# A merge projection fed with fp32 operands in place of split parts, in a two-layer hybrid encoder

## Chip, cores and metric

One core of one Trainium2 chip. The time is device microseconds of one execution of the whole two-layer trunk; runs of a kernel are summed up by their median. The engines are TensorE (PE, its weight loads shown as PEld), VectorE (DVE), ScalarE (ACT), GpSimd (POOL) and SyncE (SP), which issues most transfers.

## The reference

The trunk works on 512 tokens of width 1024. In each of two layers three branches (attention, a long convolution, gated linear attention) make 512 channels each; each branch is projected to 1024, weighted by its own sigmoid gate, and the sum is projected once more and added to the residual. Cross-attention and an MLP follow.

```python
for i in range(DEPTH):
    hn = rmsnorm(h, ln_mix[i])
    (aq, ak, av, hy, gq, gk, gv, go, glr, gates) = split_cols(hn @ w_in[i], IN_SPLITS)
    y_a = attention_mixer(aq, ak, av, attn_qnorm[i], attn_knorm[i], cos, sin) @ w_br_attn[i]
    ...
    y_b = hyena_mixer(hy, hy_conv[i], spec, hy_skip[i]) @ w_br_hyena[i]
    y_c = gla_mixer(gq, gk, gv, go, glr, gla_w_lr[i], gla_b_lr[i], gla_onorm[i]) @ w_br_gla[i]
    gate = jax.nn.sigmoid(gates.reshape(B, L, N_BRANCH, D_MODEL))
    mixed = gate[:, :, 0] * y_a + gate[:, :, 1] * y_b + gate[:, :, 2] * y_c
    h = h + mixed @ w_out[i]
```

All inputs and the output are fp32. The product that the change touches is `attention_mixer(...) @ w_br_attn[i]`: (512 x 512) by (512 x 1024).

## The kernel before

Activations lie with channels on the 128 partitions and the 512 tokens along the free axis. Nearly every large product is made of operands in two parts: `split` (lines 234 to 237) makes a high part in the format fp32r with a cast on ACT, and the rest, also fp32r, with a subtraction on DVE. `mm3` (lines 249 to 253) then accumulates three matmuls of these parts in place of one product: high by high (line 251), high weights' remainder and activations' remainder each by the other's high part (lines 252 and 253).

Weights come in chunks of 512 rows by 256 columns, stored so that a chunk is one transfer of 512 KB into a tile of 128 x 1024 fp32. Three rings of fixed tiles serve the chunks of the whole kernel in turn, in program order: 2 tiles `wr` for what a transfer brings, 3 tiles `wh` and 3 tiles `wl` for its parts (`wbuf`, line 208). `wchunk` (line 264) issues the transfer on SP and the split, the split with a priority that lies 200 steps ahead. `load` (line 256) issues other transfers on SP after the last weight transfer. `proj_cm` (line 296) runs `mm3` over the contraction tiles for one block of 128 output channels.

The work of a layer's mixing part is cut into streams: `at` attention, `gp` and `gh` gated linear attention, `hy0` and `hy1` the two halves of the long convolution, `ga0` to `ga2` the gates, `me0` to `me2` the merges of the three branches, `wo` the output projection, and others. Each stream is a generator, and `weave` (line 1136) advances them in an order written out by hand (`ORDER0`, `ORDER`, lines 145 to 156). `me0`, the merge of the attention branch, has four steps, one for each chunk of weights; three stand among the steps of the convolution and one late, before the merge of the convolution. That is the program order. From it, from the priorities (`AHEAD`, `LATE`) and from its own costs the framework plans the order of the instructions on each engine when the kernel is built.

`attention` (line 425) ends for each pair of heads with a tile of 128 channels by 512 tokens: the sum over the parts of the values into `op` (line 576), the reciprocal sums of the softmax turned round on PE (line 587), a multiplication on DVE (line 589), and a split into `yah` and `yal` (line 591, through lines 235 and 236). `merge` (line 1101) takes the four split tiles, projects them chunk by chunk, and multiplies by the gates on DVE.

```python
BUFS = dict(rb=1, mr=4, gate=8, po=1, p=4, pt=4, op=2, xk=2, xv=2, kvb=3, kvs=6, sw=3, xn=16, h8=8, y=11,
        s12=12, wraw=3, f8=8, ab4=1, F=4, g=14, st=7, wr=2, wh=3, wl=3, tiny=18, vec=2, rn=4, row=1, xg=1, w12=1,
...
    mm(out, lh, rh, start=start, stop=False, skip_group_check=True)
    mm(out, lh, rl, start=False, stop=False, skip_group_check=True)
    mm(out, ll, rh, start=False, stop=stop, skip_group_check=True)
```

Two small products elsewhere use plain fp32 operands, the position features' network of the convolution's filters (lines 646 and 649), and so do the sums over partitions by a column of ones (line 1270 among them).

Of the kernel before, what the change touches and what calls it, by code (L numbers as in the profile page):

```python
# [18 lines left out]
P = 128  # L19
# [74 lines left out]
def laid_out(a):  # L94
# [43 lines left out]
    for s_ in range(2):  # L138
# [29 lines left out]
            kt=300, pt=100, pv=150, qt=200, xs=200, xt=35, xv=10)  # L168
# [6 lines left out]
class Trunk:  # L175
# [101 lines left out]
    def proj_mem(self, W, hp, X, own):  # L277
# [15 lines left out]
                    self.mm3(ps[mt], X[kt][0][..., tk], X[kt][1][..., tk], hi[:, k], lo[:, k], kt == 0, kt == 7)  # L293
        return ps

    def proj_cm(self, ps, w, cols, X):
        n = len(X)
        for kt in range(n):
            hi, lo = w[kt // 4]
            self.mm3(ps, hi[:, kt % 4, cols], lo[:, kt % 4, cols], X[kt][0], X[kt][1],  # L300
                     kt == 0, kt == n - 1)
# [123 lines left out]
    def attention(self, l):  # L425
        nc, W = self.nc, self.I["w_in"][l]
# [33 lines left out]
        w = self.wchunk(W, CKV)  # L460
# [17 lines left out]
        for j in range(2):  # L478
            w = self.wchunk(W, CQ + j)
# [16 lines left out]
        for t in range(NT):  # L496
            qt = q[t].rearrange("p (h d) -> p h d", d=64)
            nc.vector.tensor_tensor(qt, qt, sc[:, 8 * t:8 * t + 8].unsqueeze(2).to_broadcast([P, 8, 64]),
                                    op=ALU.mult)
# [14 lines left out]
        for g in range(2):  # L514
            K2 = KS[g]
            for hh in range(4):
# [22 lines left out]
                for tp in range(2):  # L539
# [12 lines left out]
                    for kp in range(2):  # L552
# [8 lines left out]
                        for k in range(2):  # L561
                            kt = 2 * kp + k
# [7 lines left out]
                    if tp == 0:  # L570
                        yield
                if h % 2 == 0:
                    opair = self.t("op", name="op")
                tmp = self.t("st", name="ot")
                nc.scalar.copy(tmp[64:128], po[64:128])
                nc.vector.tensor_tensor(opair[r], po[0:64], tmp[64:128], op=ALU.add)
                if h % 2 == 1:

                    rs = self.tiny(2 * NT, "rs").rearrange("p (t e) -> p t e", e=2)
                    nc.vector.reciprocal(rs, sums)  # L580
                    wide = self.t("st", (P, NT, 2, 64), F32, "wide")
                    self.engs("aw")[0].tensor_copy(wide.rearrange("p t e d -> p (t e) d"),
                                                   rs.rearrange("p t e -> p (t e)").unsqueeze(2).to_broadcast([P, 8, 64]))
                    pb = self.ps("b")
                    for t in range(NT):
                        with self.late("ab"):
                            nc.tensor.transpose(pb[:, t * P:(t + 1) * P],
                                                wide[:, t].rearrange("p e d -> p (e d)"), self.ident)
                    nc.vector.tensor_tensor(opair, opair, pb, op=ALU.mult)
                    self.dump("ya", opair, lambda d, i=h // 2: d[l, i])  # L590
                    self.ya.append(self.split_new(opair, "y", name="ya"))
                yield


# [506 lines left out]
    def merge(self, l, i, W, last):  # L1101
        nc = self.nc
        y = (self.ya, self.yb, self.yc)[i]
        for mc in range(4):
            w = self.wchunk(W[l], mc, ng=1)
            for j in range(2):
                m = 2 * mc + j
                py = self.ps("mm")
                self.proj_cm(py, w, slice(j * P, (j + 1) * P), y)
                t = self.gate[i][m]  # L1110
                if i == self.first:
                    a = self.t("h8", name="acc")
                    nc.vector.scalar_tensor_tensor(a, t, 1.0, py, op0=ALU.add, op1=ALU.mult)
                    self.acc.append(a)
                else:
                    nc.vector.scalar_tensor_tensor(t, t, 1.0, py, op0=ALU.add, op1=ALU.mult)
                    nc.vector.tensor_tensor(self.acc[m], self.acc[m], t, op=ALU.add)
                if last:
                    self.mixed.append(self.split_new(self.acc[m], "g", name="mix", lo_tag="s12"))
            yield  # L1120
# [337 lines left out]
```

## Time and profile before

| what | value |
|---|---|
| median of 3 runs | 2230.19 us (2228.43 to 2230.83) |
| the profiled execution | 2230.03 us, span 2228.3 us from the first to the last instruction |
| PE busy | 2181.0 us, 98% of the span, 11032 matmuls |
| PE weight loads | 1824.3 us, 82% |
| DVE, ACT, POOL busy | 1532.3 us (69%), 1003.8 us (45%), 197.1 us (9%) |
| mean granted TensorE clock | 0.993 of 2.4 GHz |
| transfers | 233.55 MB, mean 105 GB/s |

Matmuls overlap in their pipeline and their ends are modelled, so the busy time of PE counts some of it twice in neighbouring records; the distance between two starts is what a matmul holds the engine for. A line number of a split or of `mm3` is that of the helper; the names of the tiles tell whose work it is.

### The profile page before, as it was taken

The page shows a single profiled execution, that of the slowest core. Times are in us where ns is not written, and L with a number is a line of the kernel's source. Part 1 is how long each engine was busy: PE and PEld are TensorE (multiplying, and loading weights), DVE is VectorE, ACT ScalarE, POOL GpSimd, SP SyncE. Part 2 cuts the span into 40 slices and gives each one's busy share as a digit, 9 for nine tenths or more (in the row PEclk, how much of TensorE's full clock was granted, in tenths as well). Part 3 has the DMA queues.
Part 4 walks back from the last instruction along what each step waited for, and adds up shares of the span by engine and source line. Part 5 has one row for each costly group of instructions (what it writes and reads, how often), then busy time and mean ns, then how long its engine had stood idle before and what let it go on. Part 6 is the DMA issues. An engine that isn't in the chain of part 4 may idle for free.

```text
span 2228.3 us, 28873 instructions
## 1 busy us (share of the span) xinstructions
PE 2181.0 (98%) x11032; PEld 1824.3 (82%) x11032; DVE 1532.3 (69%) x2615; ACT 1003.8 (45%) x1623; POOL 197.1 (9%) x193
## 2 busy tenths in 40 slices
PE   7989999999999999999999999999999999999999
PEld 5878888887788878888887978888887888888887
DVE  7799866979866656775485795658897575344445
ACT  6656844333344544443335576443333454432231
POOL 2020001000010200000060120110000101000004
PEclk9999999999999999999999999999999999999999
DMA  6432223223242333333344311242233312333332
GB/s 235 151 124 92 65 81 124 67 85 125 78 141 92 102 103 119 125 117 103 97 156 140 100 58 57 76 135 78 81 109 123 133 57 86 95 95 104 95 96 94
DMA packets 80097, 233.55 MB, mean 105 GB/s; under 512 B 9174, under 2 KB 11222, under 8 KB 79960
## 3 DMA queue, kind: packets, MB, share of 16 engines
q1 hardware_dynamic: 76792, 225.95, 31.6%
q0 software_dynamic: 3168, 5.77, 0.9%
q8 instruction: 86, 1.41, 0.3%
q14 instruction: 51, 0.42, 0.1%
HBM read 214.91 MB, written 16.78 MB: 104 GB/s over the span
## 4 chain that ended last, share of the span: by engine, by line
PE 83%; DVE 6%; ACT 3%; DMA 2%; issue 1%; ACTq 0%; DVEq 0%; SPq 0%
PE ps L251 26%; PE ps L253 25%; PE ps L252 25%; DVE wl L236 2%; PE ps L557 1%; ACT wh L235 1%; PE ps L566 1%; PE ps L568 1%; DMA wr<-in_w_in_dram 1%; PE ps L544 1%; ACT p L549 1%; DMA wr<-in_w_br_gla_dram 1%; PE ps L545 1%; PE ps L1312 0%; DVE ab L968 0%
## 5 line engine op out<-in xcount | busy, mean ns | idle before, releaser
L235 ACT CAST wh<-wr 128x1024 fp32r<-128x1024 f32 (+1 forms) x328 | 341.6, 1042 | 518.6 <-PE ps L252 420.6
L236 DVE TENSOR_TENSOR wl<-wr,wh 128x1024 fp32r<-128x1024 f32 x324 | 402.2, 1242 | 250.9 <-ACT wh L235 245.5
L251 PE MATMUL ps<-xh,wh 128*128 128x512 f32 x1344 | 529.8, 395 | 1.7 <-ACT wh L235 1.7
L253 PE MATMUL ps<-xh,wl 128*128 128x512 f32 x1344 | 527.5, 393 | 3.3 <-DVE wl L236 3.1
L252 PE MATMUL ps<-xl,wh 128*128 128x512 f32 x1344 | 528.5, 393 | 0.0
L253 PEld LDWEIGHTS ps<-xh,wl 128*128 128x128 f32 x1344 | 253.2, 188 | 57.5 <-DVE wl L236 6.7
L251 PEld LDWEIGHTS ps<-xh,wh 128*128 128x128 f32 x1344 | 253.4, 189 | 54.4 <-ACT wh L235 2.6
L252 PEld LDWEIGHTS ps<-xl,wh 128*128 128x128 f32 x1344 | 253.5, 189 | 49.2
L253 PE MATMUL ps<-hdh,wl 128*128 128x512 f32 x512 | 199.4, 390 | 0.0
L252 PE MATMUL ps<-hdl,wh 128*128 128x512 f32 x512 | 199.4, 390 | 0.0
L251 PE MATMUL ps<-hdh,wh 128*128 128x512 f32 x512 | 199.2, 389 | 0.0
L1374 DVE TENSOR_TENSOR macc<-ps,macc 128x512 f32<-128x512 f32 x96 | 66.3, 691 | 85.4 <-PE ps L253 84.9
L251 PEld LDWEIGHTS ps<-hdh,wh 128*128 128x128 f32 x512 | 96.1, 188 | 19.9
L252 PEld LDWEIGHTS ps<-hdl,wh 128*128 128x128 f32 x512 | 96.1, 188 | 19.8
L253 PEld LDWEIGHTS ps<-hdh,wl 128*128 128x128 f32 x512 | 96.1, 188 | 19.7
L352 POOL TENSOR_TENSOR hsum<-hsum,hsq 128x512 f32<-128x512 f32 x30 | 43.3, 1445 | 602.4 <-ACT hsq L350 602.4
L251 PE MATMUL ps<-wh,xh 128*128 128x256 f32 x320 | 92.2, 288 | 0.1
L252 PE MATMUL ps<-wl,xh 128*128 128x256 f32 x320 | 91.8, 287 | 0.0
L253 PE MATMUL ps<-wh,xl 128*128 128x256 f32 x320 | 91.6, 286 | 0.0
L1358 DVE TENSOR_TENSOR rl<-rl 128x512 f32<-128x512 f32 x64 | 44.1, 689 | 63.4 <-ACT rl L1357 63.4
L1376 POOL TENSOR_TENSOR macc<-macc,rb 128x512 f32<-128x512 f32 x16 | 23.5, 1467 | 651.1 <-DVE macc L1374 651.1
L1357 ACT ACTIVATE rl<-ps 128x512 f32<-128x512 f32 x64 | 38.0, 593 | 77.8 <-PE ps L253 77.8
(402 smaller groups left out, 4312.5 us busy)
## 6 DMA issues: line engine op xcount, KB each, us to landing
wr<-in_mlp_w_dram SPq DMA_DIRECT2D x128, 512.0 KB, 3.6
wr<-in_w_in_dram SPq DMA_DIRECT2D x108, 512.0 KB, 3.7
wraw<-in_x_wv_dram SPq DMA_DIRECT2D x16, 512.0 KB, 5.8
wr<-in_x_wk_dram SPq DMA_DIRECT2D x16, 512.0 KB, 3.6
F<-ff SPq DMA_DIRECT2D x32, 256.0 KB, 3.0
F<-F SPq DMA_DIRECT2D x32, 256.0 KB, 4.6
wr<-in_w_out_dram SPq DMA_DIRECT2D x16, 512.0 KB, 3.7
wr<-in_x_wq_dram SPq DMA_DIRECT2D x16, 512.0 KB, 3.7
```

The costliest lines, as they stand in the source:

```text
L235: r = self.nc.scalar.copy(hi, src)
L236: (lo_eng or self.nc.vector).tensor_tensor(lo, src, hi, op=ALU.subtract)
L251: mm(out, lh, rh, start=start, stop=False, skip_group_check=True)
L252: mm(out, lh, rl, start=False, stop=False, skip_group_check=True)
L253: mm(out, ll, rh, start=False, stop=stop, skip_group_check=True)
L352: eng.tensor_tensor(self.hsum, self.hsum, sq, op=ALU.add)
L544: nc.tensor.matmul(s, QH[:, tk], K2, start=True, stop=False)
L545: nc.tensor.matmul(s, QL[:, tk], K2, start=False, stop=True)
L1357: nc.scalar.activation(r, ps, AF.Relu)
L1358: nc.vector.tensor_tensor(r, r, r, op=ALU.mult)
L1374: nc.vector.tensor_tensor(acc[m], ps, acc[m], op=ALU.add)
L1376: nc.gpsimd.tensor_tensor(acc[m], acc[m], rb, op=ALU.mult)
```

## The change

The attention branch's tiles are no longer split, and neither are its merge weights. The pair's tile is taken from pool "y" and handed on as it is; `merge` loads the chunk with a new function `wfull`, ordered after the last weight transfer, and passes the fp32 tile `wr` and the fp32 pair tile straight to the matmul, one call for each contraction tile. The merges of the other two branches stay as they are.

```diff
+    def wfull(self, W, n):
+
+        w = self.wbuf("wr")
+        with self.after(self.last_w):
+            self.last_w = self.nc.sync.dma_start(w, W[n, 0])
+        return w.rearrange("p (k n) -> p k n", k=4)
...
                 if h % 2 == 0:
-                    opair = self.t("op", name="op")
+                    opair = self.t("y", name="op")
...
-                    self.ya.append(self.split_new(opair, "y", name="ya"))
+                    self.ya.append(opair)
...
         for mc in range(4):
-            w = self.wchunk(W[l], mc, ng=1)
+            full = i == 0
+            w = self.wfull(W[l], mc) if full else self.wchunk(W[l], mc, ng=1)
             for j in range(2):
                 m = 2 * mc + j
                 py = self.ps("mm")
-                self.proj_cm(py, w, slice(j * P, (j + 1) * P), y)
+                if full:
+                    for kt in range(4):
+                        nc.tensor.matmul(py, w[:, kt, j * P:(j + 1) * P], y[kt], start=(kt == 0), stop=(kt == 3))
+                else:
+                    self.proj_cm(py, w, slice(j * P, (j + 1) * P), y)
```

## Rows read from the trace of the kernel before

**Rows 1.** The page: busy time by engine, and the ending chain by line.

```profile
PE 2181.0 (98%) x11032; PEld 1824.3 (82%) x11032; DVE 1532.3 (69%) x2615; ACT 1003.8 (45%) x1623; POOL 197.1 (9%) x193
...
PE ps L251 26%; PE ps L253 25%; PE ps L252 25%; DVE wl L236 2%; PE ps L557 1%; ACT wh L235 1%; PE ps L566 1%; PE ps L568 1%; DMA wr<-in_w_in_dram 1%; PE ps L544 1%; ACT p L549 1%; DMA wr<-in_w_br_gla_dram 1%; PE ps L545 1%; PE ps L1312 0%; DVE ab L968 0%
```

**Rows 2.** Stretches: length, then busy us of PE, PEld, DVE, ACT, POOL; clock, DMA.

```profile
130.00:640.00 510.00, 495.41 (x2702) 417.83 (x2701) 413.87 (x730) 248.93 (x430) 35.25 (x42) 1.00 0.30 95
...
1260.00:1740.00 480.00, 470.62 (x2516) 395.12 (x2515) 362.63 (x613) 225.58 (x381) 33.90 (x40) 0.99 0.29 91
...
200.00:300.00 100.00, 97.11 (x648) 85.66 (x647) 88.28 (x162) 75.14 (x158) 1.56 (x1) 1.00 0.25 81
470.00:570.00 100.00, 97.26 (x497) 81.70 (x495) 92.18 (x158) 33.26 (x48) 0.00 (x0) 1.00 0.32 100
```

**Rows 3.** Waits of PE, first in 130 to 640 us, then 1260 to 1740.

```profile
PE ps L695 <- ACT w3h L677: 2.9, 1, 2.9
...
PE ps L251 <- ACT wh L235: 0.3, 1, 0.3
...
PE ps L251 <- ACT wh L235: 3.1, 4, 1.5
```

**Rows 4.** Groups by line and form, PE: the merge's first of three.

```profile
L251 PE MATMUL ps<-yah,wh 128*128 128x512 f32 x64 | 25.3, 396 | 0.0
```

**Rows 5.** Timeline of PE at the second merge chunk: start, duration, instruction.

```profile
436.35 0.39 PE L251 MATMUL ps<-yah,wh 128*128 128x512 f32 x1
...
441.79 0.39 PE L251 MATMUL ps<-xh,wh 128*128 128x512 f32 x1
```

**Rows 6.** Line 646: records, shortest, median and longest in ns.

```profile
L646 PE MATMUL ps<-z,consts x4: 589/614/640, 40.1 to 796.2; 33*64 33x512 f32 x4
```

**Rows 7.** Timeline of PE around line 646 in the second layer.

```profile
795.35 0.39 PE L253 MATMUL ps<-xh,wl 128*128 128x512 f32 x1
795.67 1.07 PE L646 MATMUL ps<-z,consts 33*64 33x512 f32 x2
796.67 0.50 PE L251 MATMUL ps<-xh,wh 128*128 128x512 f32 x1
797.00 0.39 PE L252 MATMUL ps<-xl,wh 128*128 128x512 f32 x1
```

**Rows 8.** Timeline of PE at fp32 products with one moving column.

```profile
687.07 0.39 PE L253 MATMUL ps<-xh,wl 128*128 128x512 f32 x1
687.30 0.95 PE L1270 MATMUL ps<-ones,xsq 128*128 128x1 f32 x8
688.11 0.49 PE L251 MATMUL ps<-xh,wh 128*128 128x512 f32 x1
```

**Rows 9.** Splits of weights (the page), then of attention tiles (tile op).

```profile
L235 ACT CAST wh<-wr 128x1024 fp32r<-128x1024 f32 (+1 forms) x328 | 341.6, 1042 | 518.6 <-PE ps L252 420.6
L236 DVE TENSOR_TENSOR wl<-wr,wh 128x1024 fp32r<-128x1024 f32 x324 | 402.2, 1242 | 250.9 <-ACT wh L235 245.5
...
L235 ACT CAST yah<-op x8: 608/620/622, 211.8 to 1504.7; 128x512 fp32r<-128x512 f32 x8
L236 DVE TENSOR_TENSOR yal<-op,yah x8: 681/684/693, 212.4 to 1505.8; 128x512 fp32r<-128x512 f32 x8
```

**Rows 10.** Timeline of SP's queue at the second and fourth merge chunks.

```profile
423.59 0.33 SPq L268 DMA_DIRECT2D wr<-in_w_br_attn_dram  x1
426.53 5.00 SPq L268 DMA_DIRECT2D wr<-in_w_in_dram  x2
...
552.83 3.07 SPq L268 DMA_DIRECT2D wr<-in_w_br_hyena_dram  x2
```

**Rows 11.** Timeline of ACT: casts of the later load of each pair.

```profile
436.90 1.05 ACT L235 CAST wh<-wr 128x1024 fp32r<-128x1024 f32 x1
...
586.43 1.05 ACT L235 CAST wh<-wr 128x1024 fp32r<-128x1024 f32 x1 [6.74 <-PE ps L252]
```

**Rows 12.** Tile wr: time from issue to landing.

```profile
DMA to landing us min/median/max: 1.9/3.6/7.1
```

## The prediction

> **What bounds the kernel now.** I read the page's engine totals and chain first: is one engine the limit? The matrix engine (PE) is busy 98% of the span, and of the chain that ended last 76% lies on the three lines of `mm3` [rows 1]. A busy PE isn't yet a PE that does useful work all the time, so I took the table by stretches next. The attention branch's merge runs in the mixing part of each layer, which lies in 130 to 640 us and 1260 to 1740 us. There PE is busy for 495.41 of 510 us and 470.62 of 480 us, so it idles 14.6 + 9.4 = 24.0 us; VectorE (DVE) is busy 81% and 76%, ScalarE (ACT) 49% and 47% [rows 2]. The waits of PE show how small the pieces of that idle time are: the longest entry of the first stretch is 2.9 us, and a split of weights (`wh`, line 235) makes it wait 0.3 us there and 3.1 us in the second [rows 3]. So work taken from DVE or ACT can give back little, and work added to PE is paid nearly in full.
>
> **How a product of the merge is paid today.** One (128 x 128) by (128 x 512) product is three matmuls of fp32r parts: hi x hi, lo x hi and hi x lo, 64 of each over both layers [rows 4]: 4 column chunks x 2 halves x 4 contraction tiles x 2 layers = 64 products. The record of one lasts 0.39 us, but its end is modelled; what counts is the distance from start to start. The second chunk's merge starts at 436.35 us, the next work at 441.79: 24 matmuls in 5.44 us, 0.2267 us each [rows 5]. A product is 3 x 0.2267 = 0.680 us, the whole merge 64 x 0.680 = 43.5 us of PE.
>
> **What an fp32 product costs.** The trace has no 128 x 128 by 512 product of plain fp32. The nearest is line 646, fp32 operands with 512 moving columns but only 33 rows and 64 columns of weights. Its two calls left four records, so one fp32 product is two matmuls with two weight loads; the records last 589 to 640 ns [rows 6], against 389 for an fp32r one. Three prices follow:
> Lower end: the records' lengths differ by 589 - 389 = 200 ns at the same columns, so a record holds PE 0.2267 + 0.200 = 0.427 us, a product 0.853 us.
> From start to start: the pair at 795.67 us spans 1.07 us, the second record lasts 0.589, so it starts 0.48 us after the first [rows 6, 7]. The first record is 51 ns longer than the second; if that is the wait for a weight load with nothing ahead of it, 0.43 us is left, near the lower end.
> Upper end: on line 646 the surrounding stream is moved further. The start before the pair is at 795.35; without the pair the second start after it would have come 2 x 0.2267 later, at 795.80, and it comes at 797.00 [rows 7]. So the pair cost 1.20 us, with both changes between weight tiles of 64 and 128 columns in it.
> In a chunk 8 fp32 products stand in a row with the same tile as their neighbours, so the edges should mostly go away. That weight loads needn't show: fp32 products of full 128 x 128 weights by one column run in the trace, eight records in 688.11 - 687.30 = 0.81 us, 0.10 us a record, and the first of them starts 0.23 us after an fp32r matmul, on the usual beat [rows 8]. A weight load thus fits four times into a 0.43 us record. I take 0.427 to 0.440 us a record (the second allows the 13 ns by which 0.2267 us is over 512 columns at the granted 2.4 GHz), 0.87 us a product.
> Of this the Trainium skill (page "FP8 and Floating Point Precision", section "TensorE Precision Notes") says that a true fp32 product takes four passes through the array, the four combinations of high and low parts. Four passes at the measured beat would be 0.907 us and a merge dearer by 64 x 0.227 = 14.5 us, an estimate; the trace agrees with its direction, since two records that are each two beats long are four passes where `mm3` has three.
>
> **The change part by part.**
> PE: 64 x (0.87 - 0.680) = +12.2 us; by the ends of the price +11.1 (0.853) and +33 (1.20).
> Splits removed: for each of 8 chunks one cast of 1.04 us on ACT and one subtraction of 1.24 us on DVE, for each of 8 attention tiles a cast of 0.62 and a subtraction of 0.68 us [rows 9]. That is 13.3 us of ACT and 15.4 us of DVE. No PE wait ends on a split of an attention tile, and few end on a split of weights [rows 3]. Gain taken: 0. The bound of it is a part of the 24 us of idle PE; no row allows more than a quarter, 6 us, because most waits end on tiles that the change doesn't touch, the longest on `w3h`.
> The output pair of heads in pool "y" instead of "op": the same multiplication writes it (0.68 us) and now the products read it. "y" held 2 tables and 8 parts of 11 buffers, and holds 2 + 4. Price 0.
> The new wait: fp32 weights stay in one of the two `wr` buffers until the last product has read them; before, the split set the buffer free. The load of the chunk after next needs that buffer. Behind it stand, on SyncE's queue, the later weight loads and the filter loads `F<-F`, which are ordered after the last weight load; ACT's next cast waits for it, then DVE's subtraction, then PE. Take the second chunk: its load is issued at 423.59, the two loads after it at 426.53 and about 431.2 (the merged row is 5.00 us long, one issue 0.33), and the cast of the later one starts at 436.90 [rows 10, 11]. The products then start at 436.35 as now and end 8 x 0.87 = 7.0 us later, at 443.3. Only then can the load of 431.2 be issued; loads land 3.6 us after issue [rows 12]; with cast and subtraction the parts are there at 443.3 + 3.6 + 1.05 + 1.24 = 449.2. The chunk in between gives PE 24 matmuls, 5.44 us, until 448.7. Lost: some 0.5 us. After the other chunks the cover is larger: the load that would wait for the fourth is issued at about 555.6 (the second of the merged pair) and its cast starts only at 586.43 [rows 10, 11], so it can start 7 us later for nothing; round the first and third the order shows slack of the same kind. So 0.5 us a layer, +1 us. Without cover, a chunk would cost 5.9 us, 8 of them 47 us; this keeps the upper end open.
> A gain against it: the ring of 3 split weights isn't turned by these chunks, so each neighbour may be split one chunk earlier. It can't take back more than the 3.1 + 0.3 us waited for `wh` [rows 3]. I take 0.5 us.
> Sum: 12.2 + 1.0 - 0.5 = +12.7 us. The profiled execution took 2230.0 us, 1.7 us around its span; the median of the runs is 2230.2. Forecast: 2230.2 + 12.7 = 2242.9, 0.6% slower. A difference under 0.2%, 4.5 us, can't be told from none in this kernel.
>
> **The rivals.**
> A, not slower: the freed splits feed PE sooner. For: DVE is at 88% in 200 to 300 us and 92% in 470 to 570, where PE idles 2.9 and 2.7 us [rows 2]. Against: to cancel 12.2 us, half of the 24.0 us of idle PE in both mixing parts would have to close, and most waits don't pass through a removed split. With all of the 24 us back the time would be 2230 + 12 - 24 = 2218, with half 2230. It decides from 12 us recovered. Chance 4%.
> B, a small cost: the fp32 record runs at its lower end and relief of about 6 us comes back: 2230.2 + 11.1 - 6 = 2235; or less, within 4.5 us of before. Chance for within 4.5 us 5%, for +4.5 to +7.5 us 5%.
> C, the fp32 weight loads aren't hidden and each product costs 1.0 (the pair's start to the next start, 796.67 - 795.67 [rows 7]) to 1.20 us: 20.5 to 33 us, 2251 to 2263. The full-size loads of [rows 8] speak against it. Chance 8%.
> D, the pinned buffer starves the ring: 3 us a chunk is 24 us on top, 2267; it decides where the planner, which sets the order when the kernel is built, keeps filter loads behind the blocked one. For: only two `wr` buffers. Against: three split chunks lie ahead of PE. Chance 8%.
> My forecast, +7.5 to +21 us, gets 70%. Slower by over 0.2% is 5 + 70 + 8 + 8 = 91%, same 5%, faster 4%. Range: 2238 to 2252, which with a margin for a new order of instructions leaves out parts of B, C and D, about 2 in 10.
>
> **What the profile after would show.** Two fp32 records for each product, 128 on the merge's line, with starts 0.43 to 0.44 us apart and each chunk 7 us long where it took 5.44. PE's idle time in the two mixing parts still 22 to 26 us. The load after next issued at the end of a merge chunk, and at most 1 us of PE waiting for `wh` or `wl` right after. If records start 0.5 us apart or more, C is right; if the merge is at 0.43 but the time at 2255 or above, D, and the waits on `wh` would name it; if idle PE shrinks by over 6 us, A or B. What would make the prediction wrong first is the price of the fp32 record, since 0.01 us in it moves the sum by 1.3 us, and after it an order of instructions that no row of before can show.

## The result, and the profile after

The changed kernel takes 2247.57 us (median of 4 runs, 2240.67 to 2252.5), the kernel before 2229.89 us beside it: a ratio of 1.0078, interval 1.0057 to 1.0099. Five more runs of the same kernel, shown first among the experiments, give 2245.58 us and 1.0071 (1.0059 to 1.0083). So it is 16.6 to 17.7 us slower; 12.7 us were forecast, with 2238 to 2252 as the range. The profiled execution took 2247.88 us, its span is 2245.7 us, 17.4 us over that of before. Two executions of all that follow, one of the kernel before (4358.97 us) and one of before_wr4 (4071.68 us), took nearly twice as long as the others and stand in no median here.

The page, busy time by engine and the chain that ended last by line:

```profile
PE 2194.4 (98%) x10968; PEld 1813.8 (81%) x10968; DVE 1520.2 (68%) x2599; ACT 991.7 (44%) x1607; POOL 199.0 (9%) x193
...
PE ps L251 26%; PE ps L252 26%; PE ps L253 26%; PE ps L1119 2%; DMA wr<-in_w_in_dram 1%; DVE wl L236 1%; PE ps L564 1%; ACT wh L235 1%; PE ps L551 1%; PE ps L552 1%; PE ps L573 1%; PE ps L575 1%; DVE ab L975 0%; PE ps L1324 0%; ACT p L556 0%
```

Against [rows 1] PE has 64 matmuls fewer and is busy 13.4 us longer, while DVE and ACT lost 12.1 us each. With the span 17.4 us longer, PE's idle time thus rose by 4.0 us, from 47.3 to 51.3. The engine that bounds the kernel is still PE, and the new line 1119 stands on the chain.

PE's groups by line and form, the new line:

```profile
L1119 PE MATMUL ps<-op,wr 128*128 128x512 f32 x128 | 56.4, 593 | 1.6 <-ACT wh L235 0.9 <-DMA wr<-in_w_br_attn_dram 0.7
```

The timeline of PE at the second chunk of the merge, which answers to [rows 5]:

```profile
437.88 7.03 PE L1119 MATMUL ps<-op,wr 128*128 128x512 f32 x16
444.34 0.79 PE L251 MATMUL ps<-xh,wh 128*128 128x512 f32 x1
444.97 0.40 PE L252 MATMUL ps<-xl,wh 128*128 128x512 f32 x1
```

One fp32 product is two records here too, 128 for 64 products. Sixteen of them span 7.03 us, and the last of them lasts 0.593, so their starts are (7.03 - 0.593) / 15 = 0.429 us apart. A product is 0.858 us. The next matmul is listed from 444.34 on, but it is 0.79 us long: it stood behind the last record, and the beat goes on at 444.97. From 437.88 to there, less one beat for that matmul, the chunk held PE 444.97 - 437.88 - 0.227 = 6.86 us, which is 16 x 0.429. Before it was 5.44 us. All eight chunks keep this beat (0.429 us, 0.434 and 0.436 in the two that begin with a wait), so they make 8 x 1.42 = 11.4 us.

PE's idle time in the two mixing parts, from the table by stretches (length, then busy us of PE, PEld, DVE, ACT, POOL; clock, DMA):

```profile
130.00:650.00 520.00, 505.30 (x2674) 413.88 (x2674) 410.83 (x724) 245.88 (x425) 35.83 (x41) 1.00 0.30 94
1270.00:1760.00 490.00, 477.76 (x2468) 391.29 (x2467) 353.76 (x587) 217.73 (x372) 35.46 (x39) 0.98 0.28 88
```

That is 14.7 + 12.2 = 26.9 us idle, 2.9 more than the 24.0 of [rows 2]. With the 11.4 us of the products this accounts for 14.3 of the 17.4 us of this execution. The other 3.1 us are 1.1 us of idle time outside the two parts and 2.0 us by which PE is busy longer beyond the products; no row names a cause for these. The waits say what the added idle time is for. First 130 to 650 us, then 1270 to 1760 us; us in total, times, longest:

```profile
PE ps L251 <- ACT wh L235: 2.3, 3, 1.2
...
PE ps L594 <- DVE wide L589: 1.0, 1, 1.0
PE ps L1119 <- ACT wh L235: 0.9, 1, 0.9
PE ps L253 <- DVE wl L236: 0.9, 1, 0.9
...
PE ps L253 <- DVE wl L236: 1.6, 2, 1.2
PE ps L251 <- ACT wh L235: 1.5, 3, 0.8
...
PE ps L594 <- DVE wide L589: 0.9, 1, 0.9
...
PE ps L1119 <- DMA wr<-in_w_br_attn_dram: 0.7, 1, 0.7
```

PE's waits for weights (`wh`, `wl`, and `wr` where the merge reads it) sum to 7.9 us. Line 1119 reads no `wh`; a second profile of the same kernel puts that wait, at the same place, down to the transfer of its `wr`. In the kernel before, the waits for weights are 5.3 us in these parts: 0.3 and 3.1 us for `wh` [rows 3], and for `wl`, in 130 to 640, then 1260 to 1740 us:

```profile
PE ps L253 <- DVE wl L236: 0.2, 1, 0.2
...
PE ps L253 <- DVE wl L236: 1.7, 3, 0.7
```

So weights are waited for 2.6 us longer. The 1.9 us for `wide`, the softmax's reciprocals before they are turned on PE, are new. Other waits moved both ways (4.2 us in all for `ybh` and `zh` in the first layer became 0.4 us for `ybh`, while those for `ybh` and `ybl` in the second rose from 0.3 to 2.0), so the sum of idle time rises by 2.9 us, less than the sum of the new entries.

The second chunk shows how the pinned load buffer comes to be waited for. SP's queue:

```profile
444.93 0.33 SPq L268 DMA_DIRECT2D wr<-in_w_in_dram  x1
445.35 1.01 SPq L300 DMA_DIRECT2D wr<-in_w_br_attn_dram  x1
```

The cast of that load on ACT:

```profile
449.54 1.04 ACT L235 CAST wh<-wr 128x1024 fp32r<-128x1024 f32 x1 [10.72 <-DMA wr<-in_w_in_dram]
```

And PE, which comes to this chunk after the one in between:

```profile
449.06 0.39 PE L252 MATMUL ps<-xl,wh 128*128 128x512 f32 x1
450.64 0.50 PE L251 MATMUL ps<-xh,wh 128*128 128x512 f32 x1 [1.19 <-ACT wh L235]
```

The load goes out at 444.93, when the last product of the chunk has read the buffer. The cast starts 4.61 us later, where 3.6 was counted. Between the merge chunk and its next wait PE has only 20 matmuls in its order, not the 24 that were counted on, and then waits 1.19 us. In the kernel before the same load was issued five microseconds ahead of the merge [rows 10].

The third chunk of each layer shows the same picture, with the load issued when the chunk ends and a wait that ends some 5.7 us behind the chunk:

```profile
469.68 0.50 PE L251 MATMUL ps<-xh,wh 128*128 128x512 f32 x1 [0.79 <-ACT wh L235]
...
1581.60 0.50 PE L251 MATMUL ps<-xh,wh 128*128 128x512 f32 x1 [0.79 <-ACT wh L235]
```

These three waits sum to 2.8 us. The kernel before has no wait for `wh` behind a chunk of this merge. So the 2.6 us above are a net figure: 2.8 us behind merge chunks and 1.6 us for the fp32 weights of the fourth chunk in each layer are new, and of the 5.3 us of before 2.9 us, at the later merges of the second layer, are gone; the other shifts add 1 us.

### The profile page after: what moved, and what is told of

Same layout as the page of the kernel before. It is cut to its first block, busy times and chain, and to the rows that moved or that the text cites. A ratio compares the mean times of both kernels' runs of the same rounds, so it can differ in the third digit from the quotient of the medians.

```text
span 2245.7 us, 28692 instructions
## 1 busy us (share of the span) xinstructions
PE 2194.4 (98%) x10968; PEld 1813.8 (81%) x10968; DVE 1520.2 (68%) x2599; ACT 991.7 (44%) x1607; POOL 199.0 (9%) x193
## 4 chain that ended last, share of the span: by engine, by line
PE 86%; DVE 6%; ACT 3%; DMA 2%; issue 1%; POOL 0%; ACTq 0%; DVEq 0%; SPq 0%; POOLq 0%
PE ps L251 26%; PE ps L252 26%; PE ps L253 26%; PE ps L1119 2%; DMA wr<-in_w_in_dram 1%; DVE wl L236 1%; PE ps L564 1%; ACT wh L235 1%; PE ps L551 1%; PE ps L552 1%; PE ps L573 1%; PE ps L575 1%; DVE ab L975 0%; PE ps L1324 0%; ACT p L556 0%
## 5 line engine op out<-in xcount | busy, mean ns | idle before, releaser
L235 ACT CAST wh<-wr 128x1024 fp32r<-128x1024 f32 (+1 forms) x320 | 333.1, 1042 | 533.1 <-PE ps L252 414.5
L236 DVE TENSOR_TENSOR wl<-wr,wh 128x1024 fp32r<-128x1024 f32 x316 | 392.2, 1243 | 250.6 <-ACT wh L235 249.7
```

The source lines that it names most:

```text
L235: r = self.nc.scalar.copy(hi, src)
L236: (lo_eng or self.nc.vector).tensor_tensor(lo, src, hi, op=ALU.subtract)
```

## The experiments

All comparisons are with the kernel before on the same chip. A ratio of 1.0010 is 2.2 us.

**The same kernel again.** Label after_again, no edit.

> The changed kernel once more, unchanged, for the spread of its runs. Its PE records in the merge stand 0.429 us apart, so the products alone cost 64 x (0.858 - 0.680) = 11.4 us, and 6 us of its 17.7 stay to be explained. If these 6 us are waits that the pinned load buffer makes each time, five more runs lie close together near 2247. If they are stretches at half the granted clock that fall in other places from run to run, the runs spread again over some 10 us, and time and mean granted clock go together: the lower the clock, the longer the run.

2245.58 us (2241.82 to 2247.17), 1.0071 (1.0059 to 1.0083). With the first four the runs spread over 11.8 us, from 2240.67 to 2252.5. Time and mean granted clock go together: 2241.82 us at 0.996, 2245.58 and 2245.68 at 0.993, 2247.17 at 0.992, and in the first series 2240.67 at 0.994 and 2252.5 at 0.991. The kernel before does the same: its eleven runs here go from 2225.77 (0.994) to 2233.94 us (0.991). So a part of each single execution is the clock's, for both kernels, and the close first three runs of before were luck. In the five runs here 0.004 of mean clock goes with 5.3 us, some 1.3 us for 0.001. At like clock the two kernels differ all the same: at 0.993 the kernel before took 2227.55 and 2228.59 us, the changed one 2245.58 and 2245.68. The span of this profile is 2240.9 us, 12.6 over before, against 17.4 in the first. It has the waits right behind merge chunks too, four of 0.3 to 1.2 us, 3.4 us in all.

**A buffer of its own for the fp32 weights.** Label own_buffer.

```diff
-        w = self.wbuf("wr")
+        w = self.wf
...
+        self.wf = cp.tile([P, 1024], F32, name="wf")
```

> fp32 weights of the merge in a tile of their own, so that the ring of two load buffers is never held by a product. If the pinned buffer costs the missing 6 us, the time falls to 2241 to 2242. If it costs what the trace after shows as waits for weights right after the merge chunks (1.2 and 0.8 us in the first layer, none in the second), it falls by 1 to 3 us, to 2245. If it costs nothing, 2247.

2241.79 us, 1.0057 (1.0042 to 1.0071): 3.8 us under the changed kernel, though the intervals of the two ratios overlap. Its PE waits for weights, in 130 to 650 and then 1270 to 1760 us:

```profile
PE ps L253 <- DVE wl L236: 0.9, 1, 0.9
...
PE ps L251 <- ACT wh L235: 0.3, 1, 0.3
...
PE ps L253 <- DVE wl L236: 1.7, 2, 1.2
PE ps L1120 <- DMA wf<-in_w_br_attn_dram: 1.4, 1, 1.4
...
PE ps L251 <- ACT wh L235: 0.7, 2, 0.5
```

5.0 us, where the changed kernel has 7.9 (and 8.1 in its second profile). The waits for `wh` right behind merge chunks, 2.8 us in the first profile, are all gone; the 1.4 us for `wf` are the new tile's own load. The waits fall by 3 us and the time by 3.8: the pinned buffer costs about 3 us, not the whole rest.

**A fourth fp32r pass in the kernel before.** Label four_passes.

```diff
-                self.proj_cm(py, w, slice(j * P, (j + 1) * P), y)
...
+                    for kt in range(4):
+                        nc.tensor.matmul(py, wl[:, kt, cols], y[kt][1], start=(kt == 0), stop=False,
+                                         skip_group_check=True)
+                        self.mm3(py, wh[:, kt, cols], wl[:, kt, cols], y[kt][0], y[kt][1], False, kt == 3)
...
```

> The kernel before with a fourth fp32r matmul, low part by low part, added to each product of the attention branch's merge; splits and buffers stay. If PE's time is paid one to one, 64 x 0.2267 = 14.5 us are added: 2244.4. If part of it goes into idle time of PE, 2236 to 2241. Compared with the changed kernel at the same number of passes, it has the old staging: if staging is what costs the changed kernel its 6 us, this one stays at or below the changed one although its passes are dearer (0.907 against 0.858 us a product).

2240.01 us, 1.0052 (1.004 to 1.0064): 11.0 us, 3.5 less than one to one. With the same number of passes and a dearer product (0.907 us against 0.858) it is 5.6 us faster than the changed kernel. What the changed kernel pays beyond its products thus doesn't come with the work of PE alone; whether it is the way the operands reach PE or the new order of instructions, this run can't tell.

**The splits still made.** Label kept_split: the weights and the attention tiles are split as before, and nobody reads the parts.

```diff
+        with self.tc.high_priority(offset=SPLIT_AHEAD):
+            self.split(w, self.wbuf("wh"), self.wbuf("wl"))
...
+                    self.split_new(opair, "y", name="ya")
                     self.ya.append(opair)
```

> The changed kernel with the 16 splits of the merge's weights and attention tiles still made, their parts read by nobody. Puts 13.3 us of ACT and 15.4 us of DVE work back. If the removed splits gave nothing back, as forecast, the time stays within the spread of the changed kernel, 2245 to 2250. If they gave back up to the bound of 6 us, it rises to 2253.

2245.11 us, 1.0081 (1.0067 to 1.0095), the changed kernel's time within half a microsecond. The work that the change saves on ACT and DVE, 13.3 and 15.4 us by [rows 9] and 12.1 us each by the two pages, is worth nothing here. The rings of `wh` and `wl` turn as before again in this run, and that costs nothing either. In its profile the waits behind merge chunks are there again, four with 2.7 us in all.

**Three load buffers, with and without the change.** Labels third_wr (changed kernel) and before_wr3 (kernel before), one edit each.

```diff
-            s12=12, wraw=3, f8=8, ab4=1, F=4, g=14, st=7, wr=2, wh=3, wl=3, tiny=18, vec=2, rn=4, row=1, xg=1, w12=1,
+            s12=12, wraw=3, f8=8, ab4=1, F=4, g=14, st=7, wr=3, wh=3, wl=3, tiny=18, vec=2, rn=4, row=1, xg=1, w12=1,
```

> The changed kernel with three load buffers in the ring in place of two. If the pinned buffer is what costs the 4 us that a buffer of its own gave back (2245.6 to 2241.8), the third buffer gives them back as well: about 2241.8, since while one is pinned two are left, as before. If it was an accident of the new order, 2245 to 2246.

> Control for the one above: the kernel before with three load buffers. PE waits there 3.4 us in all for cast weights in the two mixing parts. If a third buffer is no gain where none is pinned, 2229 within 0.2%; if loads were late anyway, 2225 to 2227, and the gain of the third buffer in the changed kernel isn't the pinning's alone.

third_wr: 2234.62 us, 1.0019 (1.0009 to 1.0028). before_wr3: 2222.36 us, 0.9968 (0.9957 to 0.9979). Both fell, by 11.0 and 7.0 us, so the third buffer is worth something where nothing is pinned, which I hadn't expected to this size. The difference that the change makes with three buffers is 2234.62 - 2222.36 = 12.3 us, or 11.4 us by the ratios (1.0019 / 0.9968 = 1.0051): near the price of the products. The intervals leave it open by some 3 us, and so does the clock: the runs of third_wr have a median clock of 0.992, those of before_wr3 0.994, and at 1.3 us for 0.001 that is some 2.6 us of the difference. The waits for weights fit a small rest. before_wr3, in 130 to 650, then 1270 to 1760 us:

```profile
PE ps L251 <- ACT wh L235: 0.7, 1, 0.7
...
PE ps L251 <- ACT wh L235: 1.7, 2, 1.4
PE ps L253 <- DVE wl L236: 0.5, 1, 0.5
```

third_wr, the same stretches:

```profile
PE ps L253 <- DVE wl L236: 1.2, 1, 1.2
...
PE ps L251 <- ACT wh L235: 0.7, 1, 0.7
...
PE ps L251 <- ACT wh L235: 1.4, 1, 1.4
...
PE ps L253 <- DVE wl L236: 0.5, 1, 0.5
```

2.9 and 3.8 us: 0.9 us between them, where two buffers have 2.6, and in third_wr no wait for weights of 0.2 us or more stands behind a merge chunk. before_wr3 is the fastest kernel of the study.

**All three merges in fp32.** Label all_fp32; the convolution's and the linear attention's tiles stay unsplit too (their tiles also come from other or more buffers: `yb` from pool "y", and pool "sw" has 4 in place of 3).

```diff
...
-            self.yb[2 * c + j] = self.split_new(yb, "y", name="yb")
+            self.yb[2 * c + j] = yb
...
-            self.yc.append(self.split_new(sw, "y", name="yc"))
+            self.yc.append(sw)
...
-            full = i == 0
+            full = True
```

> The same change for all three merges: 192 products of fp32 operands in place of 64, 24 chunks of weights unsplit. Each product measured 0.178 us dearer, so PE's work grows by 3 x 11.4 = 34.2 us: 2263 if only that is paid and the pinned buffers cost what they cost for one branch times one (4 us: 2267), up to 2275 if they cost it three times. If freed ACT and DVE time pays at last where the convolution's chain is waited for, below 2260.

2270.56 us, 1.0186 (1.0173 to 1.02), 41.2 us over before. The products are 34.2 us of it; the waits for weights in its two mixing parts sum to 14.5 us, 9.2 over those of before. Together that is 43.4 us, 2.2 us more than measured. If the freed time of DVE and ACT gave anything back here, this run shows no more of it than that; a new order of instructions can move the time by as much.

**Two passes in the kernel before.** Label two_passes: one of the three matmuls, the one with the activations' low part, is left out, and with it that part of the computation.

```diff
-                self.proj_cm(py, w, slice(j * P, (j + 1) * P), y)
...
+                    for kt in range(4):
+                        nc.tensor.matmul(py, wh[:, kt, cols], y[kt][0], start=(kt == 0), stop=False,
+                                         skip_group_check=True)
+                        nc.tensor.matmul(py, wl[:, kt, cols], y[kt][0], start=False, stop=(kt == 3),
+                                         skip_group_check=True)
...
```

> The kernel before with the third matmul, low weights... by low activations' part left away: of each product of the attention branch's merge only high x high and low weights x high activations stay. Leaves 64 matmuls out: 64 x 0.2267 = 14.5 us less if PE's work is paid one to one, 2214.8. The fourth pass cost only 11.0 of its 14.5 us; if the missing 3.5 us are idle time of PE behind the convolution's chain that takes up added work, taking work away leaves that idle time larger, and less is gained, 8 to 12 us: 2217 to 2221.

2211.99 us, 0.9927 (0.9914 to 0.9941): 17.4 us less, more than the 14.5 us of the pass. The expectation fell, and with it the idea that the kernel before has idle time that takes up added work. From two passes to four the time grows by 28.0 us, 14.0 a pass, nearly the 14.5 of PE; three passes, the kernel before, lie 3.4 us above the line between them. The clock can be a part of it: the runs of two_passes have a median of 0.995, those of the kernel before beside them 0.993, and PE is idle nearly as long in both profiles (46.2 us against 47.3). No run settles it.

**Only the pin.** Label pin_only: the kernel before, with a small product of the raw weights behind each chunk of the merge, into a tile that nobody reads.

```diff
+            self.last_raw = raw
...
+            raw = self.last_raw
...
+                if i == 0 and j == 1:
+                    nc.tensor.matmul(self.ps("b", (P, 1)), raw[:, 3, P:2 * P], self.ones[:, 0:1], start=True, stop=True)
```

> The kernel before, plus one small fp32 matmul (128 x 128 by one column, into a tile that nobody reads) of the raw weights behind each chunk of the attention branch's merge. It pins the load buffer until the chunk's products are done, as the change does, and leaves the products and splits as they were. The 8 small matmuls cost PE 8 x 0.2 = 1.6 us. If the pinned buffer costs 4 us by itself, the time is 2229.5 + 1.6 + 4 = 2235; if pinning only hurts together with longer products, 2231.

2241.25 us, 1.0049 (1.0037 to 1.006), 11.9 us slower, twice the dearer expectation. It isn't the clean test that I wanted. The planner put the small product of the first chunk, with one matmul of the merge, far behind the others:

```profile
425.27 0.39 PE L253 MATMUL ps<-yah,wl 128*128 128x512 f32 x1
425.50 0.28 PE L1113 MATMUL ps<-ones,wr 128*128 128x1 f32 x2
```

The other matmuls of this chunk ended by 414.2 us, so its buffer stayed pinned 12 us longer than in the changed kernel, and SP could load into it, with the issue at 425.81, only then:

```profile
425.03 0.33 SPq L268 DMA_DIRECT2D wr<-in_w_br_attn_dram  x1
425.81 7.89 SPq L268 DMA_DIRECT2D wr<-in_w_in_dram  x2
```

At 431.47 PE waits 1.25 us for the cast of this load, and at the same place in the second layer, at 1541.04, 1.29 us; the kernel before has neither wait, so a pin alone makes PE wait. PE's waits for weights, with those of the small products, sum to 7.4 us against 5.3; with the small products, 1.6 us by estimate, they name 3.7 of the 11.9 us. The rest I can't assign.

**Own buffer and three others; four passes and three buffers; four buffers.** Labels own_wr3, four_wr3, before_wr4: the edits above in pairs, and `wr=4` in the kernel before.

> The changed kernel with a buffer of its own for the fp32 weights and a ring of three for the others. If three buffers already undo the pinning, it is equal to the changed kernel with three, 2234 to 2235; if a pinned third of the ring still costs something, it comes down to the kernel before with three buffers plus the price of the products, 2222.4 + 11.4 = 2233.8, or less. Both lie within 1 us: a gain of 3 us or more would say that pinning costs in a ring of three too.

> The kernel before with a fourth fp32r pass in the attention branch's merge and three load buffers. With two buffers the fourth pass cost 11.0 us of its 14.5 us of PE. If 3.5 us went into idle time of PE that more buffers close, it costs more here, up to 2222.4 + 14.5 = 2236.9; if the difference was the new order of instructions, any value from 2230 to 2240. In each case it tells what one pass is worth, with the third buffer, beside the 12.2 us of the fp32 form.

> The kernel before with four load buffers. Three gave 0.3%. If loads still come late at some places, a fourth gives 1 to 3 us more, 2219 to 2221; if three cover the way from transfer to cast, 2222 to 2223.

own_wr3: 2237.69 us, 1.0032 (1.0021 to 1.0043). It should equal third_wr and is 3.1 us slower, with overlapping intervals and a lower median clock (0.991 against 0.992). four_wr3: 2234.14 us, 1.0018 (1.0009 to 1.0026), 11.8 us over before_wr3; so with three buffers a fourth fp32r pass and the fp32 form take the same time, four_wr3 at the higher clock (0.994 against 0.992), and the 5.6 us that lay between them with two buffers are gone. before_wr4: 2236.99 us, 1.0029 (1.0017 to 1.0041), 14.6 us over before_wr3, though its PE does the same products and waits 3.2 us for weights against 2.9. By the two profiles 7.5 us of it are idle time of PE (53.4 us against 45.9) at other places, and its runs have a median clock of 0.992 against 0.994. That the planner's other order is the cause is argued and not shown. In any case a change of one number moves this kernel by up to 15 us. This bounds what may be read from a difference of 3 us between two builds: I count such a difference only where a wait in the trace names it.

## Why the prediction was right, step by step

**What bounds the kernel.** PE, as said: work added to PE was paid for, in the fp32 form and as fp32r passes (14.0 us a pass from two to four), and the splits taken from DVE and ACT gave nothing (kept_split). "Gain taken: 0" holds, and rival A falls with it.

**The price of a product.** Forecast 0.427 to 0.440 us a record, taken as 0.87 us a product and 12.2 us in all; measured 0.429, 0.858 and 11.4 us. The lower end, from the difference of two record lengths [rows 6], was nearly exact; the 13 ns that I added for the second bound aren't there. Rival C falls: sixteen records follow each other on one beat, so the weight loads are hidden. What the 1.20 us of [rows 7] hold beyond that doesn't come with full-size products in a row; that it is the change between weight tiles of different size is argued, and no run tests it. The Trainium skill (page "FP8 and Floating Point Precision", section "TensorE Precision Notes") counts four passes for a true fp32 product. The trace agrees: a product is two records of 0.429 us, each nearly two fp32r beats of 0.2267 long; if a record is two passes, one takes 0.2145 us, 5% less than that beat.

**The new wait.** This is the term that was mis-sized. I took +1.0 us for the pinned buffer and -0.5 us for earlier splits, +0.5 together. PE's waits for weights rose by 2.6 us, from 5.3 to 7.9; a buffer of its own took 2.9 us of them away (3.8 us of time), and with three load buffers only 0.9 us of added wait is left. The mechanism was the one described, at the place described: the load after next was issued at 444.93 us, at the end of the second chunk; forecast was 443.3 for a merge that starts at 436.35, and it started at 437.88. The wait was 1.19 us, not 0.5, by two differences that add and one that takes away: the cast started 4.61 us after the issue, not 3.6 (a load that is issued just in time shows every long landing to PE, and [rows 12] go to 7.1 us); PE had 20 matmuls of cover, not 24, which is 0.9 us less; and the first matmul behind needs only the cast, so the 1.24 us of the subtraction weren't waited for. The slack that I saw round the third chunk wasn't there: it cost 0.79 us in each layer. For the second chunk of the second layer the first profile shows no such wait and the second one 0.3 us. These waits stand in all three profiles of kernels that pin one of two buffers (after, after_again, kept_split) and in none of own_buffer and third_wr, so the pinned buffer is their cause. The -0.5 us shows nowhere: kept_split, which turns the rings as before, isn't slower and waits no longer for weights (6.7 us). Rival D had the right mechanism at a tenth of its price: 2.6 us over 8 chunks, not 3 us a chunk.

**The order of instructions.** I named it as what no row of before can show and gave it no term. It holds 1.9 us of new wait for `wide` and other waits that moved both ways, so that of the 2.9 us of added idle time in the mixing parts about 0.3 is left to it beside the 2.6 us for weights. With the 11.4 us of the products this makes 14.3 us of the 16.6 to 17.7 measured. The last 2.3 to 3.4 us aren't assigned; single executions scatter by more. That the total came out inside the range therefore owes something to the range's width: the products alone were sized 0.8 us too high, the wait 2.1 us too low, and some 3 us had no term.

**The bound for "no change".** I took 0.2% from three runs within 2.4 us. Twenty runs of the kernel before in the last comparison range over 7.9 us (2226.22 to 2234.07). One execution tells no difference under 8 us here; the medians of five and more runs have intervals of some 3 us to either side.

Of what the profile should show, the record's beat, the 128 records, the 7 us chunks and the load at the chunk's end came as written; idle time in the mixing parts was 26.9 us, above the 22 to 26 forecast, and the waits right behind the merge chunks, forecast at 1 us at most in all, passed 1 us in one place and came to 2.8 us over three.

## What to carry to other kernels

When an operand is handed to the engine without being copied, the buffer that brought it lives until the last product has read it: count the buffers of the ring again with that lifetime, and add one before judging the change. The price of a form that the trace doesn't hold can be read from the difference between two records of equal columns, better than from how far an isolated one moves its neighbours. And before a few microseconds are put down to a mechanism in a kernel whose order a planner makes, change something that should be neutral and see how far that alone moves the time: here it was 15 us, part of it at a lower clock.

## What the runs showed of the hardware

The granted clock of TensorE fell to half, 1.2 GHz, at different places in executions of nearly the same work. In the changed kernel it was half around the products of the linear attention in the second layer and right ahead of both first merge chunks (last numbers but two: the granted clock):

```profile
402.90:406.30 3.40, 3.40 (x18) 3.40 (x17) 1.81 (x4) 1.74 (x4) 0.00 (x0) 0.50 0.01 2
1430.30:1437.10 6.80, 6.80 (x24) 5.62 (x22) 2.80 (x6) 1.69 (x3) 0.00 (x0) 0.50 0.28 77
1515.60:1519.00 3.40, 3.40 (x18) 3.40 (x18) 1.68 (x4) 1.59 (x3) 0.00 (x0) 0.50 0.00 0
```

The same work in the kernel before, at full clock:

```profile
1423.50:1430.00 6.50, 6.50 (x37) 5.49 (x36) 2.91 (x6) 1.69 (x3) 0.00 (x0) 1.00 0.29 84
404.00:406.70 2.70, 2.70 (x27) 2.63 (x26) 2.70 (x5) 1.35 (x3) 0.00 (x0) 1.00 0.01 3
1504.00:1507.50 3.50, 3.50 (x34) 3.43 (x35) 3.50 (x7) 1.56 (x4) 0.00 (x0) 1.00 0.12 47
```

Ahead of the fall in the middle PE had waited and then run short products:

```profile
1427.70 0.62 PE L389 MATMUL ps<-consts,small 128*128 128x128 f32 x4 [0.86 <-DVE small L383]
...
1430.04 0.33 PE L251 MATMUL ps<-qdh,kdh 64*128 64x128 f32 x2
...
1432.98 0.63 PE L253 MATMUL ps<-xh,wl 128*128 128x512 f32 x1
1433.40 0.63 PE L251 MATMUL ps<-xh,wh 128*128 128x512 f32 x1
```

The kernel before ran the same sequence after a wait of 0.87 us and kept the full clock. In the middle stretch matmuls of 512 columns start 1433.40 - 1432.98 = 0.42 us apart, where 0.2267 is usual, so the 6.8 us there cost about 3.1 us. Which executions have a fall where differs: both profiles have the same mean clock, 0.993, with falls in other places, and in the longer series, 11 runs of the kernel before and 5 of the changed one, the medians are 0.992 and 0.993. So these two kernels scatter by the clock alike, and it is no cost of the change. Between other builds here the medians differ, from 0.991 (own_wr3) to 0.995 (two_passes), and a comparison of two of them holds some of that.
